# The query latent of a transformer block summed k by k into six accumulators, and its rotary angles worked out later

## Chip, cores and metric

One core of one Trainium2 chip runs the whole program. The time is device microseconds of one execution; for the kernel before there are three runs and one profiled execution.

## What is computed

The reference is one residual block on x (256 tokens x 2048). What matters here is its beginning:

```
u = rms_norm(x, norm_pre_mix);  proj = u @ w_in
q_sb, k_sb, v_sb, q_lat, kv_lat, k_r, gate_logits = split(proj)      # 1024 x3, 768, 512, 64, 4096
q  = rms_norm(q_lat, q_norm) @ w_uq;  q_nope, q_rope = q[:128], rope(q[128:], positions)
kv = rms_norm(kv_lat, kv_norm) @ w_ukv;  k_rope = rope(k_r, positions)
```

Behind it come a stick-breaking attention on q_sb, k_sb, v_sb, a latent attention on q and kv, the gates, the output projections, and a SwiGLU layer with 5632 hidden features. Everything is f32. The "query latent" is q_lat (768 features, six column blocks of 128), the "key latent" kv_lat (512, four blocks).

## The kernel before

**Products in two parts.** Every weight comes from HBM as f32 (`raw`) and is split: ScalarE copies it into a rounded f32r tile `hi` (line 101), VectorE takes `lo = raw - hi` (line 102). x is split in the same way into `xs[:, k, 0]` and `xs[:, k, 1]` (load_x, lines 108 to 118, ScalarE line 115 and VectorE line 116). One block of 128 weight columns at one k (128 of the 2048 input features, KD = 16 of them) then needs a pair of matmuls on TensorE: hi against both parts of x, 512 columns (line 164), and lo against the first part, 256 columns (line 166).

**Units.** A unit is one load of up to 128 x 1024 weights, on SP's DMA queue, with its two splits (unit, lines 88 to 104). raw, hi and lo have four buffers each, so loads and splits run at most four units ahead of TensorE. In `pair` (lines 154 to 169) a column pair of two blocks has two PSUM banks, and a unit holds 4 k of it, eight pairs of matmuls. The query latent has 3 column pairs x 4 units (units 0 to 11), the key latent 2 x 4 (units 12 to 19), the rotary key 2 (units 20 and 21, lines 362 to 367), q_sb 4 x 4 (units 22 to 37). x is loaded during the first column pair alone (load_first, lines 212 to 216), by units cut in four and then in halves.

**Folds.** When a column pair is complete, ScalarE copies the second half of its banks out (line 173) and VectorE adds the first (line 174). For the latents a square goes to GpSimd, which adds it up (lines 337 to 340), and the fold is scaled and split for the next product (ScalarE line 344, VectorE line 345, twice each). mm_pair has two buffers of two banks each; at_bank has four single banks.

**Work hooked to units.** Everything else of this stage is attached to a unit by number (at_unit, lines 144 to 152): its instructions are ordered, engine by engine, behind the last matmul and the splits of that unit. These hooks are the statistics of x (x_stats, lines 227 to 237: a square on ScalarE and an addition of 512 columns on GpSimd per two k, units 3 to 11), the constants (unit 8), the angles (angles, lines 275 to 314, some 50 small VectorE operations in eight steps with the load of the positions before the first and two sines on ScalarE in the last; units 5 to 13 and 16), x_scale (line 239, unit 18: row sums on TensorE, then a reciprocal square root on VectorE), rope_k (unit 26) and the scales of the latents (lat_scale, lines 408 to 419, units 25, 29, 32). Apart from these edges the scheduler of the language orders each engine's queue by the order of the program and by when it expects operations to be ready.

Of the kernel before, what the change touches and what calls it, by code (L numbers as in the profile page):

```python
# [10 lines left out]
F32 = mybir.dt.float32  # L11
F32R = mybir.dt.float32r
I32 = mybir.dt.int32
AF = mybir.ActivationFunctionType
ALU = mybir.AluOpType
AX = mybir.AxisListType

P = 128
D = 2048
T = 256  # L20
NH = 8
KD = D // P
# [13 lines left out]
MLA_SCALE = 192 ** -0.5  # L36
# [17 lines left out]
def block_kernel(ctx: ExitStack, tc: tile.TileContext, a: dict, out: bass.AP):  # L54
# [30 lines left out]

    streams, split_ins = {}, [None, None]

    def unit(stream, cols_n, cuts=1, first=None):
        off = streams.get(stream, 0)
        streams[stream] = off + P * cols_n  # L90
        src = a[stream][off:off + P * cols_n].rearrange("(p c) -> p c", p=P)
        raw = wp.tile([P, 1024], F32, tag="raw", name=f"raw_{stream}_{off}", bufs=4)
        hi = wp.tile([P, 1024], F32R, tag="hi", name=f"hi_{stream}_{off}", bufs=4)
        lo = wp.tile([P, 1024], F32R, tag="lo", name=f"lo_{stream}_{off}", bufs=4)
        w = cols_n // cuts
        for c in range(cuts):
            cs = slice(c * w, c * w + w)
            if first:
                first(c)
            nc.sync.dma_start(raw[:, cs], src[:, cs])  # L100
            split_ins[0] = S.activation(hi[:, cs], raw[:, cs], AF.Copy)  # L101
            split_ins[1] = V.tensor_tensor(lo[:, cs], raw[:, cs], hi[:, cs].bitcast(F32), op=ALU.subtract)  # L102
        return hi, lo
# [4 lines left out]
    def load_x(k, n):  # L108
        if k % 2 == 0:
            xT[k // 2] = slot(f"xT{k // 2}")  # L110
        x_t = xT[k // 2]
        i = k % 2
        nc.sync.dma_start(x_t[:, i:i + n], a["xT"][:, k:k + n, :])
        for i in range(i, i + n):
            S.activation(xs[:, k, 0], x_t[:, i], AF.Copy, scale=gpre[:, k:k + 1])
            V.scalar_tensor_tensor(xs[:, k, 1], x_t[:, i], gpre[:, k:k + 1], xs[:, k, 0].bitcast(F32),
                                   op0=ALU.mult, op1=ALU.subtract)
            k += 1
# [25 lines left out]
    def at_unit(u, *fns):  # L144
        hooks.setdefault(u, []).extend(fns)
# [5 lines left out]
            for fn in hooks.pop(u, ()):  # L151
                fn()

    def pair(name, stream, K, per, rhs, first=None):
        ps = mm_pair(f"{name}_ps")
        for u in range(K // per):
            cuts = (4 if u == 0 else 2) if first else 1
            hi, lo = unit(stream, per * 2 * P, cuts, first and (lambda c: first(u, c)))
            for i in range(per):
                k = u * per + i  # L160
                for j in range(2):
                    o = (i * 2 + j) * P
                    r = rhs(k)
                    TE.matmul(ps[:, j, :], lhsT=hi[:, o:o + P], rhs=r, start=k == 0, stop=False,  # L164
                              skip_group_check=True)
                    mm = TE.matmul(ps[:, j, 0:T], lhsT=lo[:, o:o + P], rhs=r[:, 0], start=False, stop=k == K - 1,  # L166
                                   skip_group_check=True)
            unit_done(mm)
        return ps

    def fold(ps, row, out_t):
        tb = tmp.tile([P, 2, T], F32, tag="t2", name="tb", bufs=6)
        S.activation(tb, ps[:, :, T:], AF.Copy)
        V.tensor_tensor(out_t, ps[:, :, 0:T], tb, op=ALU.add)
        if row is not None:
            V.tensor_tensor(out_t, out_t, row[:, None, :].to_broadcast([P, 2, T]), op=ALU.mult)
# [31 lines left out]

    xk = lambda k: xs[:, k]
    halves = lambda x: (x[:, 0], x[:, 1])  # L210

    def load_first(u, c):
        if u == 0:
            load_x(c, 1)
        else:
            load_x(4 * u + 2 * c, 2)

    r0 = const.tile([P, T], F32, tag="r", name="r0")
    r0c = const.tile([P, 2], F32, tag="r0c", name="r0c")
# [95 lines left out]

    trig_steps = angles()
    stat_steps = x_stats()
    for u in range(3, 12):
        at_unit(u, lambda: next(stat_steps, None))
    at_unit(8, constants)  # L320
    at_unit(18, x_scale)
    for u in [*range(5, 14), 16]:
        at_unit(u, lambda: next(trig_steps, None))

    lat = {}
    for nm, n in (("q", 6), ("kv", 4)):
        acc = slot(f"acc_{nm}")[:, 0]
        g = cols[f"{nm}_norm"]
        for p in range(n // 2):
            first = nm == "q" and p == 0  # L330
            ps = pair(f"lat_{nm}{p}", "w_lat", KD, 4, xk, load_first if first else None)
            s = tmp.tile([P, 2, T], F32, tag="t2", name="s", bufs=6)
            fold(ps, None, s)
            sq = tmp.tile([P, 2, T], F32, tag="t2", name="sq", bufs=6)
            S.activation(sq, s, AF.Square)
            if p == 0:
                G.tensor_tensor(acc, sq[:, 0], sq[:, 1], op=ALU.add)
            else:
                G.tensor_tensor(acc, acc, sq[:, 0], op=ALU.add)
                G.tensor_tensor(acc, acc, sq[:, 1], op=ALU.add)  # L340
            for j in range(2):
                k = 2 * p + j
                t = slot(f"lat_{nm}_{k}", F32R)
                S.activation(t[:, 0], s[:, j], AF.Copy, scale=g[:, k:k + 1])
                V.scalar_tensor_tensor(t[:, 1], s[:, j], g[:, k:k + 1], t[:, 0].bitcast(F32),
                                       op0=ALU.mult, op1=ALU.subtract)
                lat[nm, k] = t
        lat[nm] = acc

    def rope_of(raw, name):  # L350
        ps = at_bank(f"{name}_sw")
# [8 lines left out]
    for u in range(2):  # L360
        hi, lo = unit("w_kr", 1024)
        for i in range(8):
            k = u * 8 + i
# [36 lines left out]
        u1, u2 = rope_of(kraw, "k")  # L400
        V.tensor_tensor(krr, u1, u2, op=ALU.add)

    at_unit(26, rope_k)
    rlat = slot("rlat")
    rq, rkv = rlat[:, 0], rlat[:, 1]
    rkvc = const.tile([P, 2], F32, tag="rkvc", name="rkvc")
# [1 line left out]
    def lat_scale(r, sums, acc, r_x, r_x_sq, n, name, scale=None):  # L408
        v = slot(f"v_{name}").rearrange("p a b -> p (a b)")[:, :r.free_size()]
        V.scalar_tensor_tensor(v, sums(acc, name), 1.0 / n, r_x_sq, op0=ALU.mult, op1=ALU.mult)  # L410
        V.tensor_scalar_add(v, v, EPS)
        rsqrt(r, v)
        V.tensor_tensor(r, r, r_x, op=ALU.mult)
        if scale:
            V.tensor_scalar_mul(r, r, scale)

    at_unit(25, lambda: lat_scale(rq, row_sums, lat["q"], r0, r0_sq[:, 0], 768, "q", MLA_SCALE))
    at_unit(29, lambda: lat_scale(rkv, row_sums, lat["kv"], r0, r0_sq[:, 0], 512, "kv"))
    at_unit(32, lambda: lat_scale(rkvc, col_sums, lat["kv"], r0c, r0c_sq, 512, "kvc"))
    for p in range(4):  # L420
        proj_q(p)

# [399 lines left out]
def _feature_units(w, order, per):  # L822
    k = w.shape[0] // P
    u = w.reshape(k // per, per, P, w.shape[1])[..., order]
    u = u.reshape(k // per, per, P, len(order) // 256, 256)
    return np.ascontiguousarray(u.transpose(3, 0, 2, 1, 4)).reshape(-1)
# [11 lines left out]
def _lay_out(x, positions, norm_pre_mix, w_in, b_gate, q_norm, w_uq, kv_norm, w_ukv, w_o_sb, w_o_mla, w_out,  # L838
# [21 lines left out]
        "norm_pre_ffn": norm_pre_ffn.reshape(D),  # L860
        "norm_post_mix": norm_post_mix.reshape(D),
        "norm_post_ffn": norm_post_ffn.reshape(D),
        "w_lat": _feature_units(w, 3072 + ar(1280), 4),
        "w_kr": np.ascontiguousarray(kr2).reshape(-1),
        "w_q": _feature_units(w, ar(1024), 4),
        "w_k": _feature_units(w, 1024 + ar(1024), 4),
# [33 lines left out]
```

## Time and profile before

| | us |
|---|---|
| median of 3 runs | 1397.70 |
| lowest, highest | 1396.66, 1397.94 |
| the profiled execution, whole | 1397.01 |
| its span | 1395.3 |
| first matmul | 4.67 |
| query latent, first matmul to first matmul of the key latent | 4.67 to 46.04 |

The page gives each engine's busy time and, below, the span in 40 slices of 35 us with a digit for the busy share in tenths. A busy TensorE there is one with a matmul in flight, not one at its best rate; the rate is read from the starts of successive matmuls in the timeline. "Idle" in a row is the time that the engine stood still just before it, and behind the arrow is what ended it.

### The profile page before, as it was taken

How to read it: one execution, taken by the hardware profiler on the slowest of the kernel's cores; microseconds unless marked ns; L12 is line 12 of the kernel's file. 1: busy time of each engine (PE TensorE's matmuls, PEld its weight loads, DVE VectorE, ACT ScalarE, POOL GpSimd, SP SyncE). 2: the span in 40 equal slices, each digit the busy share in tenths (PEclk: the TensorE clock that was granted, in tenths of full speed). 3: DMA queues.
4: the chain of work that ended last, by engine and by line, in shares of the span. 5: the costliest groups of instructions: out<-in, count | busy, mean ns of one | idle time of the engine just before them, and what ended most of it. 6: DMA issues, size and time to landing. Idle time of an engine off the chain costs nothing.

```text
span 1395.3 us, 17558 instructions
## 1 busy us (share of the span) xinstructions
PE 1376.4 (99%) x6752; PEld 1156.1 (83%) x6752; DVE 825.4 (59%) x975; ACT 702.5 (50%) x872; POOL 56.1 (4%) x81
## 2 busy tenths in 40 slices
PE   7999999999999999999999999999999999999997
PEld 6888888888888888887888888888888888888886
DVE  7996966555565677547555555555455545444444
ACT  7564454466558655544644444444444454434343
POOL 3210000000002200000000000000000001000001
PEclk9999999999999999999999999999999999999999
DMA  7565655555556766663765666565666566666663
GB/s 245 182 211 162 198 159 163 158 170 170 167 181 210 230 195 191 191 194 120 225 190 188 187 188 193 187 187 185 199 184 191 184 201 210 194 194 196 194 189 115
DMA packets 74341, 260.86 MB, mean 187 GB/s; under 512 B 8464, under 2 KB 9616, under 8 KB 74128
## 3 DMA queue, kind: packets, MB, share of 16 engines
q1 hardware_dynamic: 72720, 254.87, 58.8%
q0 software_dynamic: 1104, 4.20, 0.9%
q8 instruction: 53, 0.87, 0.3%
q10 hardware_dynamic: 432, 0.66, 0.1%
q14 instruction: 32, 0.26, 0.1%
HBM read 257.59 MB, written 2.10 MB: 186 GB/s over the span
## 4 chain that ended last, share of the span: by engine, by line
PE 94%; DVE 3%; issue 1%; ACT 1%; DMA 0%; SPq 0%; POOL 0%; DVEq 0%; ACTq 0%
PE gu_ps L774 12%; PE gu_ps L776 11%; PE gu_ps L775 11%; PE gate_ps L164 9%; PE wd_ps L200 6%; PE wd_ps L201 6%; PE wd_ps L202 6%; PE gate_ps L166 4%; PE wo_ps L624 4%; PE k_sb_ps L164 2%; PE q_sb_ps L164 2%; PE wo_ps L625 2%; PE wout_ps L200 2%; PE wout_ps L201 2%; PE wout_ps L202 2%; PE k_sb_ps L166 1%
## 5 line engine op out<-in xcount | busy, mean ns | idle before, releaser
L731 DVE SCALAR_TENSOR_TENSOR lo_w_gu<-raw_w_gu,packed,hi_w_gu 128x1024 fp32r<-128x1024 f32 x172 | 220.9, 1284 | 212.8 <-ACT hi_w_gu L730 211.3
L730 ACT ACTIVATE hi_w_gu<-raw_w_gu,packed 128x1024 fp32r<-128x1024 f32 x172 | 197.9, 1152 | 229.3 <-PE gu_ps L775 225.6
L774 PE MATMUL gu_ps<-hi_w_gu,hs 128*128 128x512 f32 x704 | 276.5, 393 | 0.7 <-ACT hi_w_gu L724 0.7
L776 PE MATMUL gu_ps<-lo_w_gu,hs 128*128 128x512 f32 x704 | 275.1, 391 | 0.7 <-DVE lo_w_gu L725 0.7
L775 PE MATMUL gu_ps<-hi_w_gu,hs 128*128 128x512 f32 x704 | 273.4, 389 | 0.0
L164 PE MATMUL gate_ps<-xs,hi_w_gate 128*128 128x512 f32 x512 | 181.0, 398 | 0.0
L102 DVE TENSOR_TENSOR lo_w_down<-raw_w_down,hi_w_down 128x1024 fp32r<-128x1024 f32 x88 | 109.1, 1241 | 120.5 <-ACT hi_w_down L101 120.4
L101 ACT ACTIVATE hi_w_down<-raw_w_down 128x1024 fp32r<-128x1024 f32 x88 | 93.2, 1061 | 135.6 <-PE wd_ps L201 127.4
L774 PEld LDWEIGHTS gu_ps<-hi_w_gu,hs 128*128 128x128 f32 x704 | 132.2, 188 | 30.2 <-DVE ht L738 2.2
L776 PEld LDWEIGHTS gu_ps<-lo_w_gu,hs 128*128 128x128 f32 x704 | 132.2, 188 | 28.9 <-DVE lo_w_gu L725 1.4
L775 PEld LDWEIGHTS gu_ps<-hi_w_gu,hs 128*128 128x128 f32 x704 | 132.2, 188 | 26.8
L166 PE MATMUL gate_ps<-xs,lo_w_gate 128*128 128x256 f32 x512 | 143.1, 279 | 0.0
L200 PE MATMUL wd_ps<-hi_w_down,hidh 128*128 128x512 f32 x352 | 137.2, 390 | 0.0
L202 PE MATMUL wd_ps<-lo_w_down,hidh 128*128 128x512 f32 x352 | 137.0, 389 | 0.0
L201 PE MATMUL wd_ps<-hi_w_down,hidl 128*128 128x512 f32 x352 | 137.0, 389 | 0.0
L102 DVE TENSOR_TENSOR lo_w_gate<-raw_w_gate,hi_w_gate 128x1024 fp32r<-128x1024 f32 x64 | 78.8, 1237 | 68.4 <-ACT hi_w_gate L101 68.4
L164 PEld LDWEIGHTS gate_ps<-xs,hi_w_gate 128*128 128x128 f32 x512 | 96.2, 188 | 22.7
L101 ACT ACTIVATE hi_w_gate<-raw_w_gate 128x1024 fp32r<-128x1024 f32 x64 | 67.5, 1056 | 58.6 <-PE gate_ps L164 46.8
L166 PEld LDWEIGHTS gate_ps<-xs,lo_w_gate 128*128 128x128 f32 x512 | 96.5, 189 | 0.0
L200 PEld LDWEIGHTS wd_ps<-hi_w_down,hidh 128*128 128x128 f32 x352 | 66.1, 188 | 14.1 <-DVE r L652 0.3
L202 PEld LDWEIGHTS wd_ps<-lo_w_down,hidh 128*128 128x128 f32 x352 | 66.1, 188 | 13.9
L201 PEld LDWEIGHTS wd_ps<-hi_w_down,hidl 128*128 128x128 f32 x352 | 66.1, 188 | 13.5
(338 smaller groups left out, 2175.8 us busy)
## 6 DMA issues: line engine op xcount, KB each, us to landing
raw_w_gu<-in_w_gu SPq DMA_DIRECT2D x176, 512.0 KB, 3.6
raw_w_down<-in_w_down SPq DMA_DIRECT2D x88, 512.0 KB, 3.7
raw_w_gate<-in_w_gate SPq DMA_DIRECT2D x64, 512.0 KB, 3.6
raw_w_o<-in_w_o SPq DMA_DIRECT2D x32, 512.0 KB, 3.7
raw_w_out<-in_w_out SPq DMA_DIRECT2D x32, 512.0 KB, 3.6
raw_w_lat<-in_w_lat SPq DMA_DIRECT2D x16, 512.0 KB, 4.6
raw_w_q<-in_w_q SPq DMA_DIRECT2D x16, 512.0 KB, 4.1
raw_w_k<-in_w_k SPq DMA_DIRECT2D x16, 512.0 KB, 4.0
```

Source lines behind the costliest of these rows:

```text
L101: split_ins[0] = S.activation(hi[:, cs], raw[:, cs], AF.Copy)
L102: split_ins[1] = V.tensor_tensor(lo[:, cs], raw[:, cs], hi[:, cs].bitcast(F32), op=ALU.subtract)
L164: TE.matmul(ps[:, j, :], lhsT=hi[:, o:o + P], rhs=r, start=k == 0, stop=False, skip_group_check=True)
L166: mm = TE.matmul(ps[:, j, 0:T], lhsT=lo[:, o:o + P], rhs=r[:, 0], start=False, stop=k == K - 1, skip_group_check=True)
L200: TE.matmul(ps[t], lhsT=l[0][:, ts], rhs=hi[:, cs], start=k == 0, stop=False)
L201: TE.matmul(ps[t], lhsT=l[1][:, ts], rhs=hi[:, cs], start=False, stop=False)
L202: mm = TE.matmul(ps[t], lhsT=l[0][:, ts], rhs=lo[:, cs], start=False, stop=k == K - 1)
L730: split_ins[0] = S.activation(hi, raw, AF.Copy, scale=g)
L731: split_ins[1] = V.scalar_tensor_tensor(lo, raw, g, hi.bitcast(F32), op0=ALU.mult, op1=ALU.subtract)
L774: TE.matmul(ps[t][:, j], lhsT=hs[:, k, 0, ts], rhs=hi[j], start=k == 0, stop=False)
L775: TE.matmul(ps[t][:, j], lhsT=hs[:, k, 1, ts], rhs=hi[j], start=False, stop=False)
L776: mm = TE.matmul(ps[t][:, j], lhsT=hs[:, k, 0, ts], rhs=lo[j], start=False, stop=k == KD - 1)
```

## The change

The query latent no longer goes through `pair`. All six column blocks are accumulated at once: two column pairs in the two mm_pair buffers, the third in two at_bank banks. A weight unit is now one k of all 768 columns (384 KB, 16 units instead of 12), loaded beside the x of that k; the first two units are cut in three. The last two k are done column pair by column pair, and each is folded as it is complete, half by half. In `pair` and `unit` the hooks for loading x fall away. The layout of the weights in HBM follows.

All unit numbers behind the query latent are four higher than before. The statistics of x sit at every second unit, the angles at ten units from 17 to 38 instead of 5 to 16, rope_k at 40 instead of 26.

```
-    for u in range(3, 12):
+    for u in [*range(2, 17, 2), 17]:
         at_unit(u, lambda: next(stat_steps, None))
     at_unit(8, constants)
-    at_unit(18, x_scale)
-    for u in [*range(5, 14), 16]:
+    at_unit(22, x_scale)
+    for u in (17, 19, 21, 24, 26, 28, 31, 32, 34, 38):
         at_unit(u, lambda: next(trig_steps, None))
...
+    def first_products():
+        both = [mm_pair(f"lat_q{p}_ps") for p in range(2)]
+        ps = [[b[:, j] for j in range(2)] for b in both] + [[at_bank(f"lat_q2{j}_ps") for j in range(2)]]
+        order = [(k, p) for k in range(KD - 2) for p in range(3)]
+        order += [(k, p) for p in range(3) for k in range(KD - 2, KD)]
+        w = {}
+        for k, p in order:
+            if k not in w:
+                if k < 4:
+                    load_x(k, 1)
+                elif k % 2 == 0:
+                    load_x(k, 2)
+                w[k] = unit("w_lat", 768, 3 if k < 2 else 1)
+            hi, lo = w[k]
+            for j in range(2):
+                o = (2 * p + j) * P
+                TE.matmul(ps[p][j], lhsT=hi[:, o:o + P], rhs=xs[:, k], start=k == 0, stop=False, skip_group_check=True)
+                mm = TE.matmul(ps[p][j][:, 0:T], lhsT=lo[:, o:o + P], rhs=xs[:, k, 0], start=False, stop=k == KD - 1,
+                               skip_group_check=True)
+            if p == 2:
+                unit_done(mm)
+            if k == KD - 1:
+                yield ps[p]
+
+    q_products = first_products()
     for nm, n in (("q", 6), ("kv", 4)):
...
         for p in range(n // 2):
-            first = nm == "q" and p == 0
-            ps = pair(f"lat_{nm}{p}", "w_lat", KD, 4, xk, load_first if first else None)
             s = tmp.tile([P, 2, T], F32, tag="t2", name="s", bufs=6)
-            fold(ps, None, s)
+            if nm == "kv":
+                fold(pair(f"lat_{nm}{p}", "w_lat", KD, 4, xk), None, s)
+            else:
+                tb = tmp.tile([P, 2, T], F32, tag="t2", name="tb", bufs=6)
+                for j, half in enumerate(next(q_products)):
+                    S.activation(tb[:, j], half[:, T:], AF.Copy)
+                    V.tensor_tensor(s[:, j], half[:, 0:T], tb[:, j], op=ALU.add)
...
+    next(q_products, None)
...
-    at_unit(26, rope_k)
+    at_unit(40, rope_k)
...
-    at_unit(25, lambda: lat_scale(rq, row_sums, lat["q"], r0, r0_sq[:, 0], 768, "q", MLA_SCALE))
-    at_unit(29, lambda: lat_scale(rkv, row_sums, lat["kv"], r0, r0_sq[:, 0], 512, "kv"))
-    at_unit(32, lambda: lat_scale(rkvc, col_sums, lat["kv"], r0c, r0c_sq, 512, "kvc"))
+    at_unit(29, lambda: lat_scale(rq, row_sums, lat["q"], r0, r0_sq[:, 0], 768, "q", MLA_SCALE))
+    at_unit(33, lambda: lat_scale(rkv, row_sums, lat["kv"], r0, r0_sq[:, 0], 512, "kv"))
+    at_unit(36, lambda: lat_scale(rkvc, col_sums, lat["kv"], r0c, r0c_sq, 512, "kvc"))
```

## Rows read from the trace of the kernel before

**Rows 1.** The page: busy time and share of each engine, then TensorE's busy tenths and its granted clock in tenths, in 40 slices.
```profile
PE 1376.4 (99%) x6752; PEld 1156.1 (83%) x6752; DVE 825.4 (59%) x975; ACT 702.5 (50%) x872; POOL 56.1 (4%) x81
...
PE   7999999999999999999999999999999999999997
...
PEclk9999999999999999999999999999999999999999
```
**Rows 2.** The list of waits, TensorE alone, whole run, the longest: engine and line, what it waited for, us in total, times, longest.
```profile
PE lat_q_ps L164 <- DVE xs L116: 4.7, 1, 4.7
PE lat_q_ps L166 <- DVE lo_w_lat L102: 2.4, 4, 1.2
...
PE lat_kv_ps L166 <- DVE lo_w_lat L102: 0.5, 1, 0.5
PE lat_q_ps L164 <- ACT hi_w_lat L101: 0.4, 1, 0.4
```
**Rows 3.** The table by stretches: from and to, length, then busy us (instructions) of PE, PEld, DVE, ACT and POOL, granted clock, DMA share, GB/s. The query latent, and from the key latent to the end of q_sb.
```profile
4.67:46.04 41.37, 38.41 (x192) 31.34 (x193) 36.72 (x54) 29.83 (x51) 13.08 (x10) 1.00 0.76 256
46.04:122.60 76.56, 76.07 (x437) 66.33 (x436) 68.34 (x125) 38.79 (x52) 9.85 (x15) 1.00 0.56 177
```
**Rows 4.** The timeline of TensorE in the query latent: start, length in flight, engine, line, output and inputs.
```profile
4.67 0.77 PE L164 MATMUL lat_q_ps<-xs,hi_w_lat 128*128 128x512 f32 x1 [4.67 <-DVE xs L116]
...
7.37 0.63 PE L164 MATMUL lat_q_ps<-xs,hi_w_lat 128*128 128x512 f32 x1
...
8.01 0.63 PE L164 MATMUL lat_q_ps<-xs,hi_w_lat 128*128 128x512 f32 x1
...
10.99 0.50 PE L164 MATMUL lat_q_ps<-xs,hi_w_lat 128*128 128x512 f32 x1 [0.39 <-ACT hi_w_lat L101]
...
26.93 0.39 PE L164 MATMUL lat_q_ps<-xs,hi_w_lat 128*128 128x512 f32 x1
28.50 0.39 PE L166 MATMUL lat_q_ps<-xs,lo_w_lat 128*128 128x256 f32 x1 [1.18 <-DVE lo_w_lat L102]
...
31.16 0.39 PE L164 MATMUL lat_q_ps<-xs,hi_w_lat 128*128 128x512 f32 x1
32.29 0.38 PE L166 MATMUL lat_q_ps<-xs,lo_w_lat 128*128 128x256 f32 x1 [0.74 <-DVE lo_w_lat L102]
...
38.07 0.39 PE L164 MATMUL lat_q_ps<-xs,hi_w_lat 128*128 128x512 f32 x1
...
39.80 0.39 PE L164 MATMUL lat_q_ps<-xs,hi_w_lat 128*128 128x512 f32 x1
```
**Rows 5.** Loading at the start: the split that waited for the eighth transfer, in the timeline; then the table by stretches as in rows 3; then the page's row of the weight loads of 512 KB, whose last number is us from issue to landing.
```profile
8.46 0.42 ACT L101 ACTIVATE hi_w_lat<-raw_w_lat 128x256 fp32r<-128x256 f32 x1 [1.07 <-DMA raw_w_lat<-in_w_lat]
...
0.00:10.00 10.00, 5.25 (x15) 4.25 (x16) 4.01 (x10) 5.59 (x11) 3.12 (x21) 1.00 0.65 196
10.00:14.00 4.00, 3.16 (x12) 1.66 (x12) 2.97 (x7) 2.88 (x7) 0.00 (x0) 1.00 0.99 330
...
raw_w_lat<-in_w_lat SPq DMA_DIRECT2D x16, 512.0 KB, 4.6
```
**Rows 6.** What single operations take, in the timeline of VectorE: the start of the next row less that of this one is the time for which the engine is held. Then a group by line of the first 122 us: count, busy us, mean ns of one.
```profile
36.44 0.41 DVE L285 TENSOR_TENSOR a<-ang,a 128x256 f32<-128x256 f32 x1
36.77 0.28 DVE L293 TENSOR_SCALAR turn<-a 128x256 f32<-128x256 f32 x1
36.98 1.21 DVE L102 TENSOR_TENSOR lo_w_lat<-raw_w_lat,hi_w_lat 128x1024 fp32r<-128x1024 f32 x1
38.11 0.28 DVE L294 CAST posi<-turn 128x256 int32<-128x256 f32 x1
...
90.49 1.75 DVE L124 RECIPROCAL rlat<-rlat 128x256 f32<-128x256 f32 x1
...
123.04 0.96 DVE L102 TENSOR_TENSOR lo_w_uqn<-raw_w_uqn,hi_w_uqn 128x768 fp32r<-128x768 f32 x1 [1.87 <-ACT hi_w_uqn L101]
...
L101 ACT ACTIVATE hi_w_uqn<-raw_w_uqn 128x768 fp32r<-128x768 f32 x3 | 2.5, 846 | 5.2 <-PE q_sb_ps L164 3.9 <-issue 1.3
```
**Rows 7.** GpSimd's additions in the timeline, and VectorE's operations beside those of 42.25.
```profile
24.44 6.51 POOL L233 TENSOR_TENSOR ssx<-ssx,sq 128x512 f32<-128x512 f32 x4
...
42.25 4.36 POOL L233 TENSOR_TENSOR ssx<-ssx,sq 128x512 f32<-128x512 f32 x3
...
40.79 0.83 DVE L288 TENSOR_SCALAR pf<-pr 128x256 f32<-128x256 f32 x1
...
42.50 1.52 DVE L289 TENSOR_TENSOR pr<-pr,pf 128x256 f32<-128x256 f32 x1
43.94 1.52 DVE L345 SCALAR_TENSOR_TENSOR lat_q<-s,packed,lat_q 128x256 fp32r<-128x256 f32 x1
```
**Rows 8.** How late hooked work and folds come on VectorE, in its timeline: two folds of the query latent (its second and third column pair), then the splits of three units and the first operation of the query latent's scale.
```profile
38.31 0.68 DVE L174 TENSOR_TENSOR s<-lat_q_ps,tb 128x512 f32<-128x512 f32 x1
...
54.49 0.68 DVE L174 TENSOR_TENSOR s<-lat_q_ps,tb 128x512 f32<-128x512 f32 x1
...
85.06 3.49 DVE L102 TENSOR_TENSOR lo_w_q<-raw_w_q,hi_w_q 128x1024 fp32r<-128x1024 f32 x3
88.46 0.42 DVE L410 SCALAR_TENSOR_TENSOR v_q<-q_row,r_sq 128x256 f32<-128x256 f32 x1
```
**Rows 9.** The page's group of TensorE's largest user, the gate and up product, whose matmuls go through four PSUM banks in turn: count, busy us, mean ns of one.
```profile
L774 PE MATMUL gu_ps<-hi_w_gu,hs 128*128 128x512 f32 x704 | 276.5, 393 | 0.7 <-ACT hi_w_gu L724 0.7
```

More of the change, by code (lines that the diff above doesn't have):

```diff
@@ L86, in block_kernel, with unit @@
     streams, split_ins = {}, [None, None]
-    def unit(stream, cols_n, cuts=1, first=None):
+    def unit(stream, cols_n, cuts=1):
         off = streams.get(stream, 0)
@@ L97, in unit @@
             cs = slice(c * w, c * w + w)
-            if first:
-                first(c)
             nc.sync.dma_start(raw[:, cs], src[:, cs])
@@ L152, in unit_done, with pair @@
                 fn()
-    def pair(name, stream, K, per, rhs, first=None):
+    def pair(name, stream, K, per, rhs):
         ps = mm_pair(f"{name}_ps")
         for u in range(K // per):
-            cuts = (4 if u == 0 else 2) if first else 1
-            hi, lo = unit(stream, per * 2 * P, cuts, first and (lambda c: first(u, c)))
+            hi, lo = unit(stream, per * 2 * P)
             for i in range(per):
@@ L210, in block_kernel @@
     halves = lambda x: (x[:, 0], x[:, 1])
[L212 to L216, printed above, removed]
     r0 = const.tile([P, T], F32, tag="r", name="r0")
@@ L862, in _lay_out @@
         "norm_post_ffn": norm_post_ffn.reshape(D),
-        "w_lat": _feature_units(w, 3072 + ar(1280), 4),
+        "w_lat": np.concatenate([np.ascontiguousarray(w[:, 3072:3840]).reshape(-1),
+                                 _feature_units(w, 3840 + ar(512), 4)]),
         "w_kr": np.ascontiguousarray(kr2).reshape(-1),
```

## The prediction

> **What bounds the kernel now.** [...]
>
> [...] The query latent is 96 pairs of matmuls (512 columns by hi, 256 by lo). At full pace five pairs take 1.73 us by their starts (38.07 to 39.80), 0.346 each [rows 4]; I take 0.35, so 33.6 us. It ran from 4.67 to 46.04, 41.4 us [rows 3]: 7.8 us lost. [...]
>
> From 46 to 122 us VectorE is busy 68.3 of 76.6 and TensorE still loses only the 0.5: VectorE is full there, but its splits come in time [rows 3]. That is the place to watch, as the change moves work into it.
>
> **The change, part by part.** *1. k outermost.* The x tiles and weights of one k feed six pairs, 2.1 us, instead of two pairs, 0.7. Today the first pass wants all 2 MB of x and 2 MB of weights in 11 us; now every 2.1 us wants 128 KB of x and 384 KB of weights, 0.25 MB per us, which the DMA delivers from 10 us on (0.33 MB per us up to 14) [rows 5]. The first three transfers (columns, x, 256 columns) are the same, so the first matmul stays at 4.67. k = 0 and 1 are cut into eight 128 KB transfers as now; the eighth landed at 8.46 [rows 5]. Twelve pairs at 0.64 last from 4.67 to 12.35; if the pace rises at 10.99 as now, to about 11.7. k = 2 needs 1.6 MB landed; 1.96 MB had moved by 10.0 [rows 5], but several transfers share the engines, so I put its last byte at 10.3; then hi (0.8) and lo (0.9) [rows 6]: 12.1. A wait of 0 to 0.6. Later k (0.52 MB) come 1.6 us apart at 0.33, faster than TensorE's 2.1. So q ends near 12.1 + 84 x 0.35 = 41.5 instead of 46.04: **4.5 us gained**. The same cover decides it: per two k VectorE needs 2 x 0.88 (lo of 768: 0.96 in flight, 0.08 less held, as at 1024) + 2 x 0.40 (x) + 1.1 (one statistics addition) = 3.7 of 4.2 us, ScalarE 2 x 0.85 + 2 x 0.45 + 0.6 = 3.2 [rows 6]. If VectorE's cover went (all 3.7 stretched by 15%), each two k would cost 0.06 us, 0.4 in all. SP issues 20 weight transfers instead of 18 for q, at 0.33 to 0.43 us, and waits for buffers anyway: nothing. A buffer now holds 2.1 us of work, so four of them give 8.5 us of lead instead of 11.3, against 4.6 us to landing for the old 512 KB [rows 5]: still covered. Matmul and weight-load counts are unchanged.
>
> *2. The angles, the position load and the scales placed later.* The ten hooks run eight steps (the last two find the generator empty): 28 scalar operations of 0.21 and 22 of two tensors at 0.33 [rows 6], 13.1 us of VectorE without stretching, moved from units 5 to 12 of the old count to 17 to 32 of the new (16 q units instead of 12). Leaving them out frees VectorE where the two big gaps were; with the first 0.5 us wait of the key latent that is counted as **0.5 us** beyond part 1. The position load stays on ScalarE's queue, one issue.
>
> *3. What VectorE then owes.* From 37.4 (the unit-16 split done) to the start of unit 34 at 41.5 + 18 x 2.82 + 1.6 (row sums) = 93.9, VectorE has 56.5 us. Owed, if all runs when its hook is reached: 18 splits at 1.13 = 20.5; three q folds at 1.46 and two kv folds at 1.38 = 7.2; eight GpSimd additions at 0.55 and the last statistics 1.55 = 5.95; angles 13.1; the three scales 4.4 + 4.0 + 4.0 (each one reciprocal of 1.75 and eight to twelve small operations [rows 6]); take_k 0.7; two q_sb folds 2.4. Sum 62.3: **5.8 short**. But the traced order defers such work: the q scale, hooked behind unit 25, ran its first operation behind the splits of units 26 to 28, and q2's fold came 8.5 us, three units, behind its last matmul [rows 8]. With three units of deferral the worst point (unit 33) is 54.0 owed of 53.2: 0.8 short. Bounds 0 and 5.8; I take **0.7 lost**, by the row of the same hook.
>
> *4. Three folds at once.* q's three column pairs now finish within 8 pairs of matmuls, 2.8 us from the first to the last, instead of 11 us from one to the next. The next pair of banks (kv0) is the one that the first fold frees. Folded in time: some 0.4 on ScalarE and 0.4 on VectorE for each half, as 256 columns take [rows 6], overlapped, about 1.2 us in the 2.8. The old folds were later: q1's ended its columns near 35.0 and was read at 38.31, q2's at 46.0 and read at 54.49 [rows 8]; with such delays TensorE would wait 1.2 or 6.2 us. Those had 11 us to spare and stood behind four prefetched splits; now two splits at most can stand ahead, since the last two units hold two of four buffers until the end. I take 0, bounds 0 and 6.2.
>
> Sum: 4.5 + 0.5 - 0.7 - 0 = **4.3 us**. The profiled execution took 1397.01 us (span 1395.3 and 1.7 around it), 0.7 below the median of 1397.70; 1397.0 - 4.3 = 1392.7, or 1393.4 against the median. I forecast 1393.0.
>
> [...] The six accumulators lie in six PSUM banks, taken in turn. Today's largest user of TensorE already goes through four banks in turn (two t, two halves) and keeps 393 ns in flight per 512 columns at the upper clock, as the query latent's 0.39 [rows 1, 4, 9]. [...]
>
> **Rivals.** *A. VectorE becomes the bound beside kv and q_sb*: part 3 without deferral, 5.8 lost: 4.5 + 0.5 - 5.8 = -0.8, so about 1398. For it: VectorE is full there already [rows 3], and waits inside a full queue move on. Against: 3 units of deferral in both traced places, and 46 to 122 us lost only 0.5. Chance 0.13, with partial cases about 1395 to 1397.
> *B. The bank wait*: part 4 at 1.2 to 6.2 us, TensorE idle at the first kv matmul near 41.5; above 4.3 the change is slower than before (1398.9 at 6.2). It decides by where q0's fold stands on VectorE: behind two splits it is free, behind five it is not. Chance 0.11.
> *C. The clock falls*: if the six-bank turn put the pairs from 12 us on back to 0.64, 84 x 0.29 = 24 us are lost against part 1, 1417; more than 15 such pairs cancel the gain. [...] The rows with four banks speak against it. Chance 0.02.
> *D. The start is not cured*: landings limit k = 2 to 5 and cost 2 to 3 us: 1395.2. For it: in the first 10 us only 0.2 MB per us moved [rows 5]. Chance 0.08.
> That the order does not come out as written (operations are queued by readiness, as the late folds show) would leave the angles early: 1 to 2 us less gain, inside the range.
>
> **Numbers.** The forecast's case has 0.66. A measurement of this kernel tells 0.2%, 2.8 us, from no change. Faster by more needs a gain over 2.8: nearly all of the forecast's case and a little of the others, 0.68; between, the rest of A, B and D, 0.26; slower by more needs C, or A and B together, 0.06. Best end: no loss in 3 (0.7), the pace rising early (about 1), pairs at 0.346 (0.3): 1392.7 - 2.0 = 1390.7, say 1391.0. Other end, reaching into A, B and D: 1397.2.
>
> **What would show it.** Right: 96 q pairs from 4.67 to 41 to 42, no gap over 0.6 after 13 us; the first kv matmul directly behind the last q one; VectorE busy over nine tenths from 40 to 110; TensorE waiting on lo splits below 1.5 us there. Wrong: a wait of kv0 on s or tb (B); waits on lo_w_lat, lo_w_kr or lo_w_q between units 22 and 35 (A); pairs 0.64 apart after 13 us (C); waits on raw_w_lat through hi at k = 2 to 5 (D).

## The result: 2.4 us slower, outside the range

The changed kernel takes 1399.93 us (median; lowest 1398.34, highest 1401.28) beside 1397.49 for the kernel before in the same series (1395.84 to 1398.66): a ratio of 1.0015, 95% interval 1.0009 to 1.0021. The forecast was 1393.0, with a range up to 1397.2. The profiled execution took 1399.75 us, span 1398.0, against 1397.01 and 1395.3 before.

The page of the changed kernel hardly differs from [rows 1]; only TensorE's first slices do:

```profile
PE 1377.3 (99%) x6752; PEld 1159.2 (83%) x6752; DVE 824.0 (59%) x980; ACT 704.2 (50%) x877; POOL 58.3 (4%) x81
...
PE   8989999999999999999999999999999999999997
...
PEclk9999999999999999999999999999999999999999
```

The first slice went from 7 to 8, the third from 9 to 8: something was gained early and lost between 70 and 105 us. The list of TensorE's waits from 4 to 176 us (engine and line, waited for, us in total, times, longest) says what. Against [rows 2], all waits inside the latents are gone and one new one has come:

```profile
PE q_sb_ps L163 <- DVE lo_w_q L100: 5.3, 1, 5.3
PE lat_q_ps L336 <- DVE xs L114: 4.8, 1, 4.8
```

TensorE's timeline at the two places (start, length in flight, line, tile; in brackets the idle time before and what ended it):

```profile
41.45 0.28 PE L337 MATMUL lat_q_ps<-xs,lo_w_lat 128*128 128x256 f32 x1
41.57 0.40 PE L161 MATMUL lat_kv_ps<-xs,hi_w_lat 128*128 128x512 f32 x1
...
70.71 0.40 PE L161 MATMUL q_sb_ps<-xs,hi_w_q 128*128 128x512 f32 x1
76.43 0.58 PE L163 MATMUL q_sb_ps<-xs,lo_w_q 128*128 128x256 f32 x1 [5.32 <-DVE lo_w_q L100]
76.81 0.63 PE L161 MATMUL q_sb_ps<-xs,hi_w_q 128*128 128x512 f32 x1
77.24 0.41 PE L163 MATMUL q_sb_ps<-xs,lo_w_q 128*128 128x256 f32 x1
77.45 0.63 PE L161 MATMUL q_sb_ps<-xs,hi_w_q 128*128 128x512 f32 x1
```

The key latent begins at 41.57, directly behind the query latent, where it was 46.04 before; q_sb begins at 70.71 instead of 75.69: 5.0 us ahead. Then the lo matmul of the very first q_sb pair waits 5.32 us, and the pairs behind it start 0.64 apart instead of 0.35. The table by stretches (as [rows 3]) shows the clock there:

```profile
4.78:41.57 36.79, 36.79 (x192) 31.73 (x193) 29.28 (x39) 26.25 (x45) 8.74 (x5) 1.00 0.89 287
60.00:70.00 10.00, 10.00 (x60) 8.74 (x59) 9.90 (x25) 4.49 (x7) 0.00 (x0) 1.00 0.39 138
70.00:80.00 10.00, 4.68 (x18) 3.78 (x17) 10.00 (x30) 2.84 (x6) 4.29 (x10) 0.77 0.23 62
80.00:90.00 10.00, 10.00 (x53) 8.78 (x53) 7.54 (x12) 3.18 (x3) 0.00 (x0) 0.89 0.78 252
```

The granted clock is 0.77 in 70 to 80 and 0.89 in 80 to 90. Summed over the matmuls behind the wait, the starts lie 2.7 us further apart than at full pace. So 5.0 us ahead, less 5.3 idle, less 2.7 slow: 3.0 behind. q_n begins at 125.29 instead of 122.08, k_sb at 174.69 instead of 171.89, and 2.7 is the difference of the spans. All of it is lost between 70 and 83 us: from the first k_sb matmul to the end the two executions take 1223.3 and 1223.4 us.

Why the split came at 75.16 is read on VectorE (with "..." for the operations left out, which are more of the same three kinds), and ScalarE's half of that unit stands below it:

```profile
64.18 1.22 DVE L100 TENSOR_TENSOR lo_w_kr<-raw_w_kr,hi_w_kr 128x1024 fp32r<-128x1024 f32 x1
65.31 0.42 DVE L291 TENSOR_TENSOR turn<-turn,pr 128x256 f32<-128x256 f32 x1
65.65 0.42 DVE L233 TENSOR_SCALAR vx<-x_row 128x256 f32<-128x256 f32 x1
...
66.72 1.75 DVE L122 RECIPROCAL r<-r 128x256 f32<-128x256 f32 x1
68.38 0.23 DVE L279 TENSOR_SCALAR pf<-pr 128x256 f32<-128x256 f32 x1
68.53 0.41 DVE L123 TENSOR_TENSOR newton<-r 128x256 f32<-128x256 f32 x1
...
71.01 0.68 DVE L171 TENSOR_TENSOR s<-lat_kv_ps,tb 128x512 f32<-128x512 f32 x1
...
74.83 0.41 DVE L280 TENSOR_TENSOR pr<-pr,pf 128x256 f32<-128x256 f32 x1
75.16 1.21 DVE L100 TENSOR_TENSOR lo_w_q<-raw_w_q,hi_w_q 128x1024 fp32r<-128x1024 f32 x1
```

```profile
61.48 1.06 ACT L99 ACTIVATE hi_w_q<-raw_w_q 128x1024 fp32r<-128x1024 f32 x1 [0.96 <-ACT lat_kv L367]
```

The hi half of the unit was done at 62.5, so neither load nor ScalarE was late. VectorE is never idle from 65.31 to 75.16 and runs no split: the angles (L279 to L291), the scale of x (L233 to L240 with the reciprocal square root, L122 to L126) and the second key-latent fold (L171, L368) take turns, 9.85 us. The split stands behind them in its queue.

### The profile page after: what moved, and what is told of

Its sections match the earlier page's. It is cut to its first block, busy times and chain, and to the rows that moved or that the text cites. A ratio compares the mean times of both kernels' runs of the same rounds, so it can differ in the third digit from the quotient of the medians.

```text
span 1398.0 us, 17587 instructions
## 1 busy us (share of the span) xinstructions
PE 1377.3 (99%) x6752; PEld 1159.2 (83%) x6752; DVE 824.0 (59%) x980; ACT 704.2 (50%) x877; POOL 58.3 (4%) x81
## 4 chain that ended last, share of the span: by engine, by line
PE 95%; DVE 3%; ACT 0%; issue 0%; DMA 0%; POOL 0%; DVEq 0%; SPq 0%; ACTq 0%
PE gu_ps L800 11%; PE gu_ps L798 11%; PE gu_ps L799 11%; PE gate_ps L161 9%; PE wd_ps L197 6%; PE wd_ps L198 6%; PE wd_ps L199 6%; PE gate_ps L163 4%; PE wo_ps L648 4%; PE q_sb_ps L161 2%; PE k_sb_ps L161 2%; PE wo_ps L649 2%; PE wout_ps L197 2%; PE wout_ps L198 2%; PE wout_ps L199 2%; PE lat_q_ps L336 2%
## 5 line engine op out<-in xcount | busy, mean ns | idle before, releaser
L99 ACT ACTIVATE hi_w_gate<-raw_w_gate 128x1024 fp32r<-128x1024 f32 x64 | 67.5, 1056 | 58.2 <-PE gate_ps L161 46.4
```

## The experiments

**What can be told apart.** O, the order: what counts is the longest stretch of VectorE's queue in which no split stands, set against how far TensorE is ahead. L, the load: VectorE is too full, wherever the steps stand. Each kernel ran beside the kernel before; ratios are to that. e1 to e12 ran in three later series, in which its medians were 1397.77 to 1398.01. Places (us of the first matmul) are from the profiled execution of each:

| kernel | query latent | angle steps | key latent begins | q_sb | k_sb | us | ratio (95%) |
|---|---|---|---|---|---|---|---|
| before | column pairs | beside q | 46.04 | 75.69 | 171.89 | 1397.49 | 1 |
| after | k outermost | beside kv, kr, q_sb | 41.57 | 70.71 | 174.69 | 1399.93 | 1.0015 (1.0009, 1.0021) |
| e1 | k outermost | none | 41.70 | 70.69 | 166.43 | 1391.56 | 0.9953 (0.9941, 0.9966) |
| e2 | k outermost | behind most of q_sb | 42.51 | 71.50 | 169.26 | 1394.45 | 0.9975 (0.9965, 0.9986) |
| e3 | k outermost | beside q | 48.06 | 77.26 | 173.22 | 1398.67 | 1.0006 (0.9997, 1.0015) |
| e4 | column pairs | beside kv, kr, q_sb | 45.87 | 74.48 | 172.55 | 1397.49 | 0.9996 (0.9987, 1.0005) |
| e12 | column pairs | behind most of q_sb | 46.30 | 74.92 | 172.58 | 1398.13 | 1.0001 (0.9992, 1.0010) |

**e1, no angles.**

```
     def angles():
-        ... (50 operations in eight steps)
+        G.memset(trig, 0.5)
+        yield
```

> The changed kernel without the VectorE, ScalarE and position-load work of the angles (cos and sin are filled with a constant by GpSimd, so that part of the computation is left out). Theory O (order): TensorE's wait of 5.3 us at the first q_sb unit comes from VectorE's queue, in which two chains (angles, x_scale) and a fold fill 9 us between two splits; with one chain gone the splits slip in between as before, no wait over 0.5 us up to 120 us, and no slow pairs behind it: 5.3 + 2.6 less, about 1392.0, 5.5 below the kernel before. Theory L (load): VectorE simply has too much to do before the first q_sb split; 13 us less of it also ends the wait, about the same. Both would fall if the wait stays over 2 us.

1391.56 us, 0.9953 (0.9941 to 0.9966). TensorE has no wait behind 13 us at all before k_sb, and its lead at k_sb is 5.5 us. The angles are what the new wait needs; without them k outermost keeps all that it gains. Between O and L this run doesn't decide: both expected it.

**e2, all angle steps behind most of q_sb.**

```
-    for u in (17, 19, 21, 24, 26, 28, 31, 32, 34, 38):
+    for u in (36, 38, 40, 42, 44, 45, 46, 47):
-    at_unit(40, rope_k)
+    at_unit(50, rope_k)
```

> The changed kernel with the eight angle steps at units 36, 38, 40, 42, 44, 45, 46, 47 and rope_k at 50, beside the last q_sb units and the first products of the latents. Theory O: in the queue as built no 4.4 us of VectorE work stand between two splits before the key products, so the gain of the k-outermost order stays: 1392.5, with the first key-latent matmul at 41.6 and waits of TensorE below 1 us up to 160 us. Theory L: the 13 us are owed 30 us later; if load decides, a wait of 2 to 5 us turns up between 110 and 150 us: 1395 to 1397.

1394.45 us, 0.9975 (0.9965 to 0.9986): between the two expectations, and faster than both kernels. No wait at q_sb, and q_n begins at 117.45, 4.6 ahead. But at k_sb the lead is 2.6. Two stretches of the table, and TensorE's first q_r matmul:

```profile
120.00:130.00 10.00, 10.00 (x58) 8.68 (x57) 10.00 (x23) 4.87 (x7) 0.00 (x0) 1.00 0.53 157
130.00:140.00 10.00, 9.08 (x51) 7.69 (x51) 9.93 (x24) 6.58 (x9) 0.00 (x0) 1.00 0.59 198
```

```profile
135.50 0.47 PE L161 MATMUL qr_ps<-lat_q,hi_w_uqr 128*128 128x512 f32 x1 [0.92 <-ACT hi_w_uqr L99]
```

VectorE (third of the busy times) is full for 20 us there, and TensorE loses 2.0 us from q_n to k_sb. That is the part in which L holds. At k_sb the angles cost 8.3 us in the changed kernel (174.69 against 166.43 in e1) and 2.8 here (169.26), of which 0.8 was lost at the start of this execution (key latent at 42.51). That the full VectorE is the cause of the 2.0 is read from the table; e10 below, with five steps there instead of eight, has no wait at q_r and takes 49.85 us from q_n to k_sb, as the kernel before (49.81).

**e3, k outermost with the angles where they had been.**

```
-    for u in (17, 19, 21, 24, 26, 28, 31, 32, 34, 38):
+    for u in [*range(9, 18), 20]:
```

> The k-outermost part alone: angle hooks at units 9 to 17 and 20, four later than before, so as many units ahead of q_sb as before; scales as changed. Theory O: the longest stretch without a split is 2.8 us beside q_sb and 5.4 at one of the last query-latent units; no wait at q_sb, at most 2 us at the end of the query latent: 1393 to 1395. Theory L: all the work of before is owed by the first q_sb split, 5 us earlier than before, so 4 to 5 us of waits turn up before 72 us: 1397 or more.

1398.67 us, 1.0006 (0.9997 to 1.0015). The number is L's, and so is the amount of waiting, but the place is neither's. TensorE, then ScalarE, then the waits of SP's queue from 12 to 45 us, and that queue's timeline:

```profile
33.93 0.79 PE L336 MATMUL lat_q_ps<-xs,hi_w_lat 128*128 128x512 f32 x1 [4.66 <-DVE xs L114]
```

```profile
32.85 0.91 ACT L113 ACTIVATE xs<-xT,packed 128x256 fp32r<-128x256 f32 x2 [2.55 <-DMA xT<-in_xT]
```

```profile
SPq L98 <- DVE lo_w_lat L100: 12.2, 9, 2.3
...
SPq L98 <- DVE a L273: 2.4, 1, 2.4
```

```profile
14.42 0.42 SPq L111 DMA_DIRECT2D xT<-in_xT  x1
15.05 13.68 SPq L98 DMA_DIRECT2D raw_w_lat<-in_w_lat  x8
28.78 0.43 SPq L111 DMA_DIRECT2D xT<-in_xT  x1
```

TensorE waits 4.66 us for a split of x; that x (k = 10 and 11) was issued only at 28.78, because eight weight loads (k = 8 to 15) stand in front of it in SP's queue, from 15.05 on. They waited for raw buffers, that is for lo splits of earlier units: 2.3 us at most, and the last one 2.4, until the lo split at 27.42 was done (the list names L273, the operation behind it); ahead of that split VectorE ran two angle operations (L271 and L272, from 26.03). In the changed kernel two weight loads stand there between one load of x and the next (x at 13.94, 17.64, 21.27 and 24.91). So moving the hooks also changed the order of SP's queue; why the scheduler wrote it so, the runs don't show. It is again a queue that runs as written, one step further back: the eighth weight load was issued by 28.73 (15.05 + 13.68), that x at 28.78. e9 tests this.

**e4, the new hooks with the old query latent.**

```
-    for u in [*range(5, 14), 16]:
+    for u in (13, 15, 17, 20, 22, 24, 27, 28, 30, 34):
-    at_unit(26, rope_k)
+    at_unit(36, rope_k)
```

> The later angle hooks alone: the kernel before with its pair by pair query latent, angle hooks four units lower than in the change (13, 15, 17, 20, 22, 24, 27, 28, 30, 34) and rope_k at 36. Theory O: the same two chains meet, 7.6 us without a split stand ahead of the first q_sb split, so a wait of 3 to 5 us there and some 2 us of slow pairs, against 2.4 us won in the query latent: 1399 to 1401. Theory L: TensorE reaches q_sb 5 us later than in the change, so VectorE has its time and there is no wait: 1395.

1397.49 us, 0.9996 (0.9987 to 1.0005): between. The stretch without a split is there with the old query latent too:

```profile
65.88 1.22 DVE L102 TENSOR_TENSOR lo_w_kr<-raw_w_kr,hi_w_kr 128x1024 fp32r<-128x1024 f32 x1
67.01 0.28 DVE L288 TENSOR_SCALAR pf<-pr 128x256 f32<-128x256 f32 x1
...
75.33 1.21 DVE L102 TENSOR_TENSOR lo_w_q<-raw_w_q,hi_w_q 128x1024 fp32r<-128x1024 f32 x1
```

```profile
76.60 0.39 PE L166 MATMUL q_sb_ps<-xs,lo_w_q 128*128 128x256 f32 x1 [1.73 <-DVE lo_w_q L102]
```

Both expectations were missed, O's wait of 3 to 5 us and L's 1395. 8.3 us without a split cost a wait of 1.73 alone, as q_sb starts at 74.48 here, 3.8 us later than in the changed kernel. The split comes at 75.33, there at 75.16: the lead was spent on reaching the same late split sooner. And behind this shorter wait the pairs are 0.35 apart.

**e5, the wait filled.**

```
+    fillers = at_bank("fill")
+    for i in range(15):
+        TE.matmul(fillers, lhsT=lat["q", 0][:, 0, 0:P], rhs=xs[:, 0], ...)
+        TE.matmul(fillers[:, 0:T], lhsT=lat["q", 0][:, 0, 0:P], rhs=xs[:, 0, 0], ...)
     for p in range(4):
         proj_q(p)
```

> The changed kernel, with 30 matmuls more on TensorE between the key-rope product and the first q_sb product (15 pairs of the size used everywhere, 15 x 0.353 = 5.3 us, into a bank that nothing reads): they fill the wait for the first q_sb split, so that TensorE doesn't idle there. Theory S (split and clock): the split lands at about 75.2 as before, the 5.3 us are spent on the fillers in place of idle time, and the pairs behind it are 0.353 apart at once, where the changed kernel had nine at 0.64: 9 x 0.29 = 2.6 us less than the changed kernel, about 1397.3, with q_n beginning at 122.7 in place of 125.3. Theory M (the pairs behind the wait are slow because their splits come late, not by the clock): pairs still 0.6 apart behind the fillers, and the time stays at 1399.9. If the fillers only delay what follows (no wait is there to be filled): 1399.9 + 5.3 = 1405.

1398.15 us, 1.0003 (0.9994 to 1.0011): 1.8 below the changed kernel in the medians, where S had 2.6 and M 0. TensorE around the end of the fillers:

```profile
76.59 0.39 PE L161 MATMUL q_sb_ps<-xs,hi_w_q 128*128 128x512 f32 x1
77.30 0.39 PE L163 MATMUL q_sb_ps<-xs,lo_w_q 128*128 128x256 f32 x1 [0.32 <-DVE lo_w_q L100]
77.52 0.39 PE L161 MATMUL q_sb_ps<-xs,hi_w_q 128*128 128x512 f32 x1
77.75 0.28 PE L163 MATMUL q_sb_ps<-xs,lo_w_q 128*128 128x256 f32 x1
77.87 0.40 PE L161 MATMUL q_sb_ps<-xs,hi_w_q 128*128 128x512 f32 x1
```

The pairs are 0.35 apart at once. From the first lo matmul to q_n it takes 46.4 us (77.30 to 123.73), in the changed kernel 48.9 (76.43 to 125.29): 2.4 less, which is the price of the fallen clock alone (granted 1.00 here in 70 to 80 and 80 to 90, 0.77 and 0.89 there). At q_n 1.6 of it are left in the profiled executions, since in this one the key latent began 0.8 later (42.40), after a wait of 1.01 at 11.90 for a hi split whose load was late.

**e6, only the order changed.**

```
-    at_unit(22, x_scale)
+    at_unit(26, x_scale)
```

> The changed kernel with the one step that computes the row scale of x (reciprocals, reciprocal square roots) hung on unit 26 in place of 22; nothing is added or taken away. Theory O (order on VectorE): in the order that the scheduler writes, the stretch without a split moves from ahead of the first q_sb split to ahead of the splits of the sixth and seventh q_sb unit (8.2 and 6.3 us of operations, summed from single durations), where 0.3 us are left ahead of the first: no wait at the first q_sb unit, first q_sb pairs 0.353 apart from 70.7 on, and a wait of 3 to 7 us at a later q_sb unit between 85 and 100, with slow pairs behind it. Time within 2 us of the changed kernel, 1398 to 1402. Theory L (load: VectorE is too full in 64 to 76, whatever the order): the wait stays at the first q_sb unit, only shorter by the x-scale's 3 to 4 us, and the time falls to 1395 or 1396.

1400.51 us, 1.0015 (1.0006 to 1.0024), with no operation added or removed. q_sb begins at 69.44 and runs five units without a wait; then:

```profile
88.03 0.39 PE L163 MATMUL q_sb_ps<-xs,lo_w_q 128*128 128x256 f32 x1 [3.01 <-DVE lo_w_q L100]
...
88.96 0.62 PE L161 MATMUL q_sb_ps<-xs,hi_w_q 128*128 128x512 f32 x1
...
89.59 0.63 PE L161 MATMUL q_sb_ps<-xs,hi_w_q 128*128 128x512 f32 x1
...
95.39 0.39 PE L163 MATMUL q_sb_ps<-xs,lo_w_q 128*128 128x256 f32 x1 [2.52 <-DVE lo_w_q L100]
```

The waits stand at the sixth and seventh q_sb unit, the two that O named from the order of the queue, and slow pairs behind both. L's 1395 or 1396 is excluded. This run decides between the two for the place of the wait. For its length it doesn't: the two waits add up to 5.53 us, beside 5.32 in the changed kernel, and VectorE is full up to them (the third busy time; this run, then the changed kernel):

```profile
45.00:95.00 50.00, 44.86 (x248) 38.81 (x247) 49.59 (x102) 27.60 (x42) 14.77 (x18) 0.97 0.48 149
45.00:80.00 35.00, 29.68 (x160) 25.57 (x159) 34.73 (x71) 19.02 (x31) 14.03 (x18) 0.93 0.45 138
```

A backlog of VectorE that the order only moves from one unit to another is not excluded.

**e7 and e8, three angle steps early, five late.**

```
-    for u in (36, 38, 40, 42, 44, 45, 46, 47):      # e2
+    for u in (11, 12, 13, 38, 40, 42, 44, 46):      # e7
+    for u in (7, 9, 11, 38, 40, 42, 44, 46):        # e8
```

> The changed kernel with the angle steps on units 11, 12, 13 (where VectorE had 3 of 10 us free in the q latent) and 38, 40, 42, 44, 46, and the key's rotation on unit 50. Longest stretch of VectorE without a split in its order: 4.0 us of operations, beside the last q_sb units. Theory O (order): no wait of more than 0.5 us in q, kv, kr and q_sb; q_n begins at 117.5; of the 2 us that the angles behind q_sb alone gave back beside q_n, q_r and k_n half stays away, since three of eight steps are gone from there: 1392.5 to 1393.8. Theory L (load: VectorE's total up to k_n is what counts, wherever the steps stand): 1394.5, as with all angles behind q_sb. If steps 11 to 13 hold up the splits of w_lat as in the kernel with the angles beside the q latent: a wait of 1 to 4 us at 30 to 40 and 1396 to 1399.

> As the kernel with three early and five late angle steps, the early ones on units 7, 9, 11 in place of 11, 12, 13. Longest stretch without a split in VectorE's order in the q latent: 3.5 us ahead of the split of its tenth unit, against 1.7 us there for 11, 12, 13. Theory O (order, and a raw buffer that comes free only by that split): VectorE was 10.00 of 10 us busy in 20 to 30, so the split comes late by 2 to 3 us, and as weight loads and x loads share one queue, a wait of 1 to 3 us appears at a unit between 28 and 38 for a split of x or of w_lat; 1 to 3 us slower than 11, 12, 13, that is 1394 to 1397. Theory L (load): the same time as 11, 12, 13 within 0.5 us.

1397.82 us, 0.9997 (0.9988 to 1.0006), and 1400.08 us, 1.0016 (1.0007 to 1.0025). The favoured expectation for e7 was missed by 4 us, the third one for it held: waits of 2.92 and 0.73 us for splits of x, at 36.16 and 42.89. e8 waits 4.69 us at 30.06, more than expected. e8's time is 3 us above its range; the step from e7 to e8, 2.3 us, is inside the 1 to 3 expected. Stretches of VectorE alone were too small a view: the waits are for splits of x, as in e3. In SP's queue seven weight loads stand in front of the late x in e7 (issued at 29.36) and eight in e8. e10 tests that cause for e7; for e8 it is read from the order of the queue alone, in which SP waits for lo splits ten times from 15 to 50 us, 20.2 us in all and 5.8 at most.

**e9, e3 with the loads of x moved forward in SP's queue.**

```
...
                 elif k % 2 == 0:
+                    for c in {4: (4,), 6: (6, 8), 8: (10, 12), 10: (14,)}.get(k, ()):
+                        fetch_x(c, 2)          # the load; load_x(k, 2) keeps the splits alone
                     load_x(k, 2)
```

> The kernel with k outermost and the angles where they stood before the change (beside the q latent), with one thing moved: the loads of x from chunk 8 on are put into the queue of loads two to four weight units earlier, so that they no longer stand behind weight loads that wait for a raw buffer. Nothing else moves by hand. Theory Q (queue: in the kernel without this the 4.66 us wait for a split of x came from a load of x that stood behind a weight load, which waited for the low split of an earlier unit, which stood behind angle operations on VectorE): the wait of 4.66 us goes, the clock stays at 1.00 in 30 to 40, the key latent begins at 41.5 to 43 in place of 48.06, and the time falls from 1398.7 to 1392 to 1394.5. Theory V (VectorE itself is too full beside the q latent with the angles there): the wait stays at 3 us or more, for a low split of w_lat in place of one of x, and the time stays above 1396.5.

1395.36 us, 0.9985 (0.9976 to 0.9994), 3.3 below e3. The wait for x is gone and from 13 us to the end of the query latent TensorE's longest wait is 0.25; so the cause given for e3, the place of x in SP's queue, holds. But the time is 0.9 above Q's range, and the key latent begins at 44.93:

```profile
44.93 0.47 PE L163 MATMUL lat_kv_ps<-xs,hi_w_lat 128*128 128x512 f32 x1 [1.95 <-DVE s L361]
```

```profile
41.82 1.22 DVE L100 TENSOR_TENSOR lo_w_lat<-raw_w_lat,hi_w_lat 128x1024 fp32r<-128x1024 f32 x1
42.96 0.42 DVE L293 TENSOR_TENSOR turn<-turn,pr 128x256 f32<-128x256 f32 x1
43.29 0.42 DVE L361 TENSOR_TENSOR s<-lat_q_ps,tb 128x256 f32<-128x256 f32 x1
...
44.36 0.42 DVE L361 TENSOR_TENSOR s<-lat_q_ps,tb 128x256 f32<-128x256 f32 x1
```

That is the prediction's rival B, in a kernel that the prediction was not about: the first q fold stands behind splits and angle operations, and the key latent waits 1.95 us for its banks, with slow pairs behind it (granted clock 0.83 in 40 to 50).

**e10 and e11, e7 and e2 with the loads of x moved forward likewise.**

> The kernel with three angle steps on units 11, 12, 13 and five behind, with the loads of x moved forward in the queue as in the kernel before. Theory Q: the waits of 2.92 and 0.73 us for splits of x go, with the slow pairs behind the first; the key latent begins at 41.5 to 42.5 in place of 47.22; as the angles behind q_sb are five steps in place of eight, less is given back beside q_n to k_n than the 2 us of the kernel with all eight there: 1392 to 1393.5. Theory V: waits for low splits of w_lat of 2 us or more take their place, 1395 or more.

> The kernel with all angles behind most of q_sb, with the loads of x moved forward in the queue: a control. No wait for x stood in that kernel's q latent, so all theories expect the same time, 1394.4 within 0.7. If the early loads of x by themselves gain or cost (weights come later by about 1 us at 14 to 20), it shows here.

e10: 1393.42 us (1392.96 to 1396.16), 0.9972 (0.9962 to 0.9982), 4.4 below e7 in the medians and 3.5 by the ratios. The waits for x are gone and the time is in Q's range. The key latent of the profiled execution (1394.68) is not: it begins at 44.84, behind a wait of 1.84 us at the start, with slow pairs after it, and one of 0.70 for the first fold. e11: 1393.98 us, 0.9972 (0.9962 to 0.9982), inside the 0.7 given for the control. Both beat the kernel before by some 4 us and the changed kernel by 6; between e10, e11 and e2 these runs don't decide.

**e12, the missing cell: column pairs with the angles behind.**

```
-    for u in [*range(5, 14), 16]:
+    for u in (32, 34, 36, 38, 40, 41, 42, 43):      # same work as 36 to 47 with k outermost
-    at_unit(26, rope_k)
+    at_unit(46, rope_k)
```

> The kernel before the change (column pairs one after another in the q latent) with its angle steps where the kernel with all angles behind q_sb has them (same work units, q_sb's last eight): the cell that is missing between the two orders of the q latent and the places of the angles. Against that kernel it differs by k outermost alone. Theory O: the key latent begins at about 45.9, as in the kernel with the hooks alone, 3.4 us later than with k outermost; no wait of over 1 us at q_sb; beside q_n to k_n, where VectorE is full, TensorE coming 3.4 us later waits 0 to 2 us less: 1396 to 1398, so k outermost is worth 1.5 to 3.4 us where no wait takes it back. Theory L (what counts is VectorE's total up to k_n, and the order of the q latent doesn't matter): 1394.5.

1398.13 us, 1.0001 (0.9992 to 1.0010), 0.1 above O's range; L's 1394.5 is excluded. Against e2 k outermost is worth 3.7 us here: the key latent begins 3.8 earlier, and at k_sb 3.3 are left.

## Why the prediction was wrong, point by point

**Part 1, k outermost (4.5 us gained): right.** The key latent begins at 41.57 instead of 46.04, 4.47 earlier. Expected end of the query latent 41.5. e2 beside e12 gives 3.7 for it in the whole time. Its pair of 0.64 is 7.37 to 8.01 in [rows 4], its 1.1 for a statistics addition 1.44 in [rows 7] less 0.33 in [rows 6], and part 3's 0.55 is 0.83 less 0.28 there.

**Part 2, angles out of the query latent (0.5): right.** Its two big gaps are the waits of 1.18 and 0.74 in [rows 4]. The lead grows from 4.47 to 5.07 at the rotary key (65.06 instead of 70.13): the 0.5 us wait at the first key-latent unit is gone.

**Part 3 (0.7 lost): this is the step that failed.** It summed VectorE's work up to a late point, found 5.8 us too much if all of it runs when its hook is reached, and then wrote that "the traced order defers such work", taking three units of deferral from [rows 8]. The rows of the hook did not carry over: in the kernel before one operation of the q scale came behind three splits, and the next split 0.9 us behind it (89.35), while behind the change two chains and a fold reach VectorE together. The queue as written then holds 9.85 us of them and no split, and VectorE took no later, ready split ahead of them: that split's hi half was there at 62.5, and it ran at 75.16. The part didn't look at the first q_sb unit (26); it named unit 33 as the worst point. e6 shows that the order decides where the wait falls (it moves with one hook), e4 that the stretch is there without k outermost, e1 and e2 that it goes when the angles do.

How much is waited is near the sum that the part had set aside: 5.32 us here and 5.53 in e6, beside 5.8 without deferral (5.6, as 18 x 1.13 is 20.3 and not 20.5). In e4, where TensorE comes 3.8 later, it is 1.73. So the size fits a VectorE that owes too much by then, and that another order in the same stretch would have lost less is not shown; e2, which did, moved the angles out of it.

The term's bounds were wrong as well. The wait itself, 5.3, is inside 0 to 5.8. But a wait of that length costs more than itself, and the part had no price for that: 2.7 us of slow pairs, measured at 2.4 alone in e5. With 8.0 in place of 0.7 the sum is 4.5 + 0.5 - 8.0 = -3.0, and the spans differ by 2.7.

**Part 4 and rival B (bank wait, 0): right for this kernel**, since the key latent begins 0.12 behind the last query-latent matmul. e9 and e10 show that it was a near thing: with all angles ahead of the folds it costs 1.95 us and slow pairs, with three steps of them 0.70.

**Rival A (VectorE becomes the bound, 0.13) is what came**, by its own sign, a wait on lo_w_q between units 22 and 35 (here unit 26), and near its price, 5.8 for a wait of 5.32. Its 1398 fell short by the slow pairs behind the wait, 2.7 us at a granted clock of 0.77 and 0.89. With 0.13 for it and 0.06 for slower, the chances leaned on rows of a stretch in which the moved work did not yet stand.

**Rival C (the clock falls with six banks in turn): not here.** With six banks in turn the table has 1.00 for the whole query latent. The first nine pairs are 0.64 apart all the same (4.78 to 10.04), as at the start of the kernel before [rows 4]; from 10.63 on they are about 0.35 apart up to the end (40.51, 40.86, 41.21 start three of them), with 0.39 to 0.40 in flight for 512 columns, as the 393 ns of the four banks in [rows 9], at the granted clock of nine tenths or more in [rows 1]. Behind the start the clock fell where TensorE had stood idle for a wait: 0.77 in 70 to 80, behind the 5.32 us.

**Rival D (a start that is not cured): not in this execution**, in which no wait is left from 4.78 to 41.57. It does turn up elsewhere: the wait for a weight load at 11 to 12.4 us is 0.68, 1.84 and 0.16 in e9, e10 and e11, whose first loads are the same. In e5, with the first loads of the changed kernel, it is 1.01, and e10's nine runs lie 3.2 us apart. What makes the difference stays open.

## What to carry to other kernels

When work is moved into a stretch where an engine is already full and runs its queue as written, as VectorE did here (a split whose hi half was there at 62.5 ran at 75.16), ask first whether the sum fits without counting on deferral; here that sum, 5.8 us, was near the wait that came, 5.32. Then list what stands in the queue ahead of each operation that the bottleneck waits for, and compare the longest such stretch with the lead; that told where the wait came. Time gained ahead of a late operation is worth nothing until that operation comes earlier too, so put a moved chain where the bottleneck doesn't soon wait for what stands behind it (e2, e10), and read the DMA queue in the same way (in e3 an x stood behind eight weight loads until 28.78, and TensorE waited 4.66 us for it). Price a wait of TensorE by what follows it (2.7 us of slow pairs behind the 5.32), not by its length alone.

## What was not expected of the hardware

Behind some waits of TensorE the clock fell and behind others not. Measured as the excess of the starts behind the wait over full pace: after waits of 1.29 and 1.73 us (both in e4) 0.1 and 0.3 us, with no slow pairs in a row (granted clock 1.00 in 20 to 30 and in 70 to 90); after 1.95 (e9), 2.52 and 3.01 (e6), 2.92 (e7), 4.66 (e3), 4.69 (e8) and 5.32 (the changed kernel) 1.6, 1.7, 1.6, 1.6, 1.4, 2.9 and 2.7 us, with a granted clock of 0.83 (e9, 40 to 50), 0.71 (e6, 90 to 100), 0.83 (e7 and e3, 30 to 40), 0.69 (e8, 30 to 40) and 0.77 (the changed kernel, 70 to 80). In e6 the pairs directly behind the 3.01 us wait were still fast (88.03 to 88.84) and the slow ones came from 88.96 on, in e9 from 46.48 on, 1.5 us behind the wait. Near the start of e12 a shorter wait was enough: five slow pairs (12.73 to 15.29, granted clock 0.55 in 12 to 14 and 0.59 in 14 to 16) follow a wait of 1.50 that ended at 11.62 (and one of 0.23 at 12.35); behind one of 1.51 in the same run, which ended at 29.77, there are none (1.00 in 20 to 30 and 30 to 40). In e10 a wait of 1.84 ended at 12.40 (one of 0.49 at 13.39), and the granted clock (third number from the end) fell only at 14:

```profile
12.00:14.00 2.00, 1.11 (x5) 0.74 (x6) 1.41 (x2) 2.00 (x5) 0.00 (x0) 1.00 1.00 336
14.00:16.00 2.00, 2.00 (x10) 1.66 (x9) 1.96 (x3) 2.00 (x6) 0.66 (x1) 0.62 1.04 385
16.00:18.00 2.00, 2.00 (x9) 1.71 (x8) 2.00 (x3) 2.00 (x6) 1.00 (x1) 0.53 0.90 288
```

So the loss stood in pairs that themselves waited for nothing: from 0.9 us behind the end of the wait in e6, 1.5 in e9 and 2.4 in e10 (14.83). That the wait is the cause was tested in the changed kernel alone, by e5.
